# Two column blocks of an output projection by seven products of halves, with four sums of weights formed in DRAM during the recurrence before it

## The chip, the cores and the metric

The kernel runs on one core of one Trainium2 chip. The metric is device time in microseconds (us) of one execution; less is better. Before the change the median of three runs was 1098.96 us (1098.77 to 1100.81). Tile, line and engine names are those of the profile: PE is TensorE's matmuls, PEld its weight loads, DVE is VectorE, ACT is ScalarE, POOL is GpSimd, SP is the engine that only issues transfers. "L157" is line 157 of the kernel before.

## What is computed

One decoder layer on 512 tokens of 2048 channels. The stage that changes is the output projection with its residual; the rest is cut to a line each.

```python
h = rms_norm(x, norm_g)                      # 512 x 2048
z = h @ w_in                                 # 2048 x 6272: r, k, v, lora inputs, gates, pool input
y_rwkv = wkv7_scan(r, decay, k, v, kk, a)    # 16 heads of 64, a recurrence over the tokens
y_pool = pooled means of 2, 4, 8, 16 tokens @ w_pool
y_mix = concatenate([y_rwkv * silu(g), y_pool * scale * silu(g_pool)])   # 512 x 2048
x = x + y_mix @ w_out                        # the output projection, 2048 x 2048
x = x + sigmoid(x @ w_pg + b_pg) * (p @ w_ple)
out = rms_norm(x, final_g)
```

All is float32. The big products split each operand into a high part that TensorE multiplies exactly enough and the rest (`hi`, `lo`), and add three products: hi by hi, hi by lo, lo by hi. One "chunk" below is a 128 x 512 piece of a weight matrix, 256 KB.

## The kernel before

**Stages, in the order of time.** Norm and transposes of the input; the input projection, whose matmuls are kept in the order of the program and put between the steps of the recurrence, which goes over 8 pairs of heads with 8 "hops" each (one hop is one step of the state over 64 tokens; the state's scaled copy is `s0p`, L816, on POOL); the output projection `proj(w_out, ..., "o")`; the gate projection `proj(w_pg, ..., "g")`; the last norm.

**The weight chain.** `wsplit` (L129 to L133) loads a chunk into a tile `raw` by a transfer that SP issues, ACT copies it to `whi` (L132), and DVE subtracts for `wlo` (L133). The tiles `raw`, `whi` and `wlo` have 4 buffers each, so the load of a chunk can start when the subtraction of the chunk four places earlier has ended. SP's queue is issued in order: a load that waits for its buffer holds up all behind it.

**The output projection.** Four column blocks of 512 (`ec` 0 to 3). A block goes over the 16 chunks of the sum (`k`) in the list `order`; each chunk is used for 4 tiles of 128 tokens, three matmuls each, 12 matmuls in all of 512 columns (L157, `acc_o`). In block 0 the activations come on the way: `load_y` (L918, an ACT-issued transfer from the DRAM copy `yd`) fills one of six `yin` buffers, ACT makes `yhi` and DVE `ylo`, both whole tiles of 16 chunks. After a block, ACT-issued transfers bring the residual `x` (L994), DVE adds the four accumulators to it (L995), the sums go to DRAM (`x2d`, L996), and `turn` transposes the four tiles on PE (`px`, L1002, 16 transposes), splitting the result into `x2hi` and `x2lo`. Blocks 0, 1 and 2 are turned right behind their own matmuls, block 3 within the first gate block.

**What sets the order.** Each engine runs its own queue in order; a scheduler that records the program orders them by priorities from the program's text, with `tc.issue_after(...)` where an instruction must stand behind another and `tc.high_priority` where it may come early.

Of the kernel before, what the change touches and what calls it, by code (L numbers as in the profile page):

```python
# [9 lines left out]
F32 = mybir.dt.float32  # L10
# [5 lines left out]
P = 128  # L16
# [14 lines left out]
CK = 4  # L31


@with_exitstack
def trunk_kernel(ctx: ExitStack, tc: tile.TileContext, x, p, norm_g, w_in, mu, w0, w_up, a0, a_up,
# [87 lines left out]
    hhi = hp.tile([P, KT, T], F32R, name="hhi", tag="ahi")  # L123
    hlo = hp.tile([P, KT, T], F32R, name="hlo", tag="alo")


    def wsplit(src, kt, n, nm):
        raw = wp.tile([P, kt, n], F32, name=f"raw_{nm}", tag="raw")
        nc.sync.dma_start(out=raw, in_=src)  # L129
# [275 lines left out]
    def pool_unit(n):  # L405
# [32 lines left out]
        nc.scalar.dma_start(out=yd[NJ + m], in_=sgp)  # L438

# [316 lines left out]
    def recur(j, work, between):  # L756
# [17 lines left out]
        for ch in range(NCH):  # L774
# [25 lines left out]
            if ch < NCH - 1:  # L800
# [12 lines left out]
                if ch < NCH - 2:  # L813
                    for h in range(2):
                        hc = slice(64 * h, 64 * h + 64)
                        nc.gpsimd.tensor_scalar(s0p[hc, :], nxt[hc, hc], pcn[hc], None, ALU.mult)  # L816
# [56 lines left out]
    pending = []  # L873
    need("k", 0)
# [39 lines left out]
    AHEAD = 6  # L914

    def load_y(k):
        t_ = ymp.tile([P, T], F32, name=f"yin{k}", tag="yin", bufs=AHEAD)
        nc.scalar.dma_start(out=t_, in_=yd[k])  # L918
        split(yhi[:, k, :], ylo[:, k, :], t_)

# [6 lines left out]
    x2hi = hp.tile([P, KT, T], F32R, name="x2hi", tag="ahi")  # L927
    x2lo = hp.tile([P, KT, T], F32R, name="x2lo", tag="alo")
# [11 lines left out]
    def proj(w, hi_, lo_, ec, nm, ks=range(KT), tts=range(NT), keep=None, aside=None):  # L940
        acc = {tt: acc_tile(f"acc_{nm}{ec}_{tt}") for tt in tts}
        for i, k in enumerate(ks):
# [5 lines left out]
            elif nm == "o" and ec == 0 and i < 4:  # L948
                wh, wl = chunk(f"{nm}{ec}_{k}", 0)
            elif keep is None or LATE <= i < KT - KEEP:  # L950
                wh, wl = wsplit(src, 1, EC, f"{nm}{ec}_{k}")
            else:
# [12 lines left out]
                if i >= LATE:  # L965
                    continue
            for tt in tts if keep is None or i >= LATE else tts[:-1]:
# [3 lines left out]
            if aside is not None and i == 2:  # L971
                with tc.issue_after(e_.ins):
                    hi = aside()
                with tc.issue_after(hi.ins):
                    recall(0, lp)
# [11 lines left out]
    for ec in range(D // EC):  # L987
        es = slice(ec * EC, (ec + 1) * EC)
        acc = proj(w_out, yhi, ylo, ec, "o", order)
        x2 = []  # L990
        for tt in range(NT):
            rows = slice(tt * P, (tt + 1) * P)
            t_ = pp.tile([P, EC], F32, name=f"x2_{ec}_{tt}", tag=("u", "sw")[tt // 2])
            nc.scalar.dma_start(out=t_, in_=x[rows, es])  # L994
            nc.vector.tensor_tensor(t_, acc[tt], t_, ALU.add)  # L995
            nc.scalar.dma_start(out=x2d[rows, es], in_=t_)  # L996
            x2.append(t_)
        def turn(ec=ec, x2=x2):
            for i in range(EC // P):
                pt = psM.tile([P, T], F32, name=f"px2_{ec}_{i}", tag="m")  # L1000
                for tt in range(NT):
                    nc.tensor.transpose(pt[:, tt * P:(tt + 1) * P], x2[tt][:, i * P:(i + 1) * P], ident)  # L1002
# [178 lines left out]
```

## Time and profile before

| | |
|---|---|
| median of 3 runs | 1098.96 us |
| the profiled execution, by its own clock | 1097.72 us |
| its span in the profile | 1095.9 us |
| TensorE clock granted, mean | 0.998 |
| PE / DVE / ACT / POOL busy | 98% / 65% / 41% / 7% |
| output projection, four blocks | 728.97 to about 909 us of the span |

The span leaves out 1.8 us of the execution that lie around it. "Busy" of PE counts from the start of the first to the modelled end of the last of overlapping matmuls; a single matmul's duration is longer than the step from one to the next.

### The profile page before, as it was taken

The page shows a single profiled execution, that of the slowest core. Times are in us where ns is not written, and L with a number is a line of the kernel's source. Part 1 is how long each engine was busy: PE and PEld are TensorE (multiplying, and loading weights), DVE is VectorE, ACT ScalarE, POOL GpSimd, SP SyncE. Part 2 cuts the span into 40 slices and gives each one's busy share as a digit, 9 for nine tenths or more (in the row PEclk, how much of TensorE's full clock was granted, in tenths as well). Part 3 has the DMA queues.
Part 4 walks back from the last instruction along what each step waited for, and adds up shares of the span by engine and source line. Part 5 has one row for each costly group of instructions (what it writes and reads, how often), then busy time and mean ns, then how long its engine had stood idle before and what let it go on. Part 6 is the DMA issues. An engine that isn't in the chain of part 4 may idle for free.

```text
span 1095.9 us, 17196 instructions
## 1 busy us (share of the span) xinstructions
PE 1070.8 (98%) x6060; PEld 877.6 (80%) x6060; DVE 708.2 (65%) x1835; ACT 448.3 (41%) x917; POOL 76.9 (7%) x180
## 2 busy tenths in 40 slices
PE   5999999999999999999999999999999999999996
PEld 4888878887788888788878788888888888888885
DVE  6687867878688679678886956454433424445366
ACT  7633535345335335353343344543222222233337
POOL 2100110110110110100101101000000000000000
PEclk9999999999999999999999999999999999999999
DMA  7433433332423333333334242775534438455534
GB/s 233 116 96 97 111 92 84 96 100 73 120 82 105 104 92 89 96 82 93 91 94 119 79 138 93 232 233 169 172 124 136 167 99 244 137 189 137 181 106 154
DMA packets 178486, 138.56 MB, mean 126 GB/s; under 512 B 34678, under 2 KB 139743, under 8 KB 178399
## 3 DMA queue, kind: packets, MB, share of 16 engines
q1 hardware_dynamic: 157694, 103.89, 32.1%
q10 hardware_dynamic: 20704, 33.56, 9.8%
q8 instruction: 48, 0.79, 0.3%
q14 instruction: 40, 0.32, 0.1%
HBM read 118.02 MB, written 18.87 MB: 125 GB/s over the span
## 4 chain that ended last, share of the span: by engine, by line
PE 86%; DVE 5%; DMA 4%; ACT 3%; issue 1%; SPq 0%; ACTq 0%; DVEq 0%
PE acc_o L157 16%; PE zb L157 14%; PE acc_g L157 14%; PE zv L157 8%; PE zk L157 7%; PE zg L157 7%; PE zr L157 7%; PE py L157 2%; PE pple L157 2%; PE pm L157 1%; PE pu L157 1%; DMA n<-nd 1%; PE pp L157 1%; DMA raw_g<-in_w_pg_dram 1%; PE ps L157 1%
## 5 line engine op out<-in xcount | busy, mean ns | idle before, releaser
L133 DVE TENSOR_TENSOR wlo_g<-raw_g,whi_g 128x512 fp32r<-128x512 f32 x84 | 57.0, 685 | 79.6 <-ACT whi_g L132 76.5
L157 PE MATMUL zb<-hhi,whi_b 128*128 128x512 f32 x256 | 107.0, 418 | 0.0
L133 DVE TENSOR_TENSOR wlo_o<-raw_o,whi_o 128x512 fp32r<-128x512 f32 x64 | 43.9, 690 | 91.4 <-ACT whi_o L132 91.4
L157 PE MATMUL zb<-hhi,wlo_b 128*128 128x512 f32 x256 | 100.5, 393 | 0.0
L157 PE MATMUL acc_o<-whi_o,ylo 128*128 128x512 f32 x256 | 100.2, 391 | 0.0
L157 PE MATMUL acc_o<-whi_o,yhi 128*128 128x512 f32 x256 | 99.9, 390 | 0.0
L157 PE MATMUL zb<-hlo,whi_b 128*128 128x512 f32 x256 | 99.9, 390 | 0.0
L157 PE MATMUL acc_o<-wlo_o,yhi 128*128 128x512 f32 x256 | 99.8, 390 | 0.0
L132 ACT CAST whi_g<-raw_g 128x512 fp32r<-128x512 f32 x84 | 51.9, 620 | 102.7 <-PE acc_g L157 55.4
L157 PE MATMUL acc_g<-whi_g,x2hi 128*128 128x512 f32 x208 | 81.3, 391 | 0.0
L157 PE MATMUL acc_g<-wlo_g,x2hi 128*128 128x512 f32 x208 | 80.9, 389 | 0.0
L157 PE MATMUL acc_g<-whi_g,x2lo 128*128 128x512 f32 x208 | 80.7, 389 | 0.0
L132 ACT CAST whi_o<-raw_o 128x512 fp32r<-128x512 f32 x64 | 39.9, 623 | 97.0 <-PE acc_o L157 96.7
L816 POOL TENSOR_SCALAR s0p<-sbd,pw 64x64 f32<-64x64 f32 x96 | 56.6, 589 | 322.8 <-DVE sbd L809 255.0
L132 ACT CAST whi_b<-raw_b 128x512 fp32r<-128x512 f32 x64 | 39.7, 621 | 86.5 <-PE zv L157 35.4
L133 DVE TENSOR_TENSOR wlo_b<-raw_b,whi_b 128x512 fp32r<-128x512 f32 x64 | 43.8, 685 | 34.2 <-ACT whi_b L132 32.9
L157 PEld LDWEIGHTS zb<-hhi,wlo_b 128*128 128x128 f32 x256 | 48.0, 188 | 11.1
L661 DVE TENSOR_TENSOR xw<-xw,tm 128x60 f32<-128x60 f32 (+24 forms) x248 | 52.1, 210 | 6.8
L157 PEld LDWEIGHTS acc_o<-wlo_o,yhi 128*128 128x128 f32 x256 | 48.1, 188 | 10.3 <-DVE wlo_o L133 0.4
L157 PEld LDWEIGHTS acc_o<-whi_o,yhi 128*128 128x128 f32 x256 | 48.1, 188 | 9.7
L157 PEld LDWEIGHTS acc_o<-whi_o,ylo 128*128 128x128 f32 x256 | 48.1, 188 | 9.8
L157 PEld LDWEIGHTS zb<-hhi,whi_b 128*128 128x128 f32 x256 | 48.2, 188 | 8.5
(285 smaller groups left out, 2550.0 us busy)
## 6 DMA issues: line engine op xcount, KB each, us to landing
raw_b<-in_w_in_dram SPq DMA_DIRECT2D x64, 256.0 KB
raw_o<-in_w_out_dram SPq DMA_DIRECT2D x64, 256.0 KB
raw_g<-in_w_pg_dram SPq DMA_DIRECT2D x64, 256.0 KB
raw_k<-in_w_in_dram SPq DMA_DIRECT2D x32, 256.0 KB
raw_r<-in_w_in_dram SPq DMA_DIRECT2D x32, 256.0 KB
raw_v<-in_w_in_dram SPq DMA_DIRECT2D x32, 256.0 KB
raw_g<-in_w_in_dram SPq DMA_DIRECT2D x32, 256.0 KB
n<-nd SPq DMA_DIRECT2D x16, 256.0 KB
```

Source lines behind the costliest of these rows:

```text
L132: nc.scalar.copy(hi, raw)
L133: nc.vector.tensor_tensor(lo, raw, hi.bitcast(F32), ALU.subtract)
L157: i = nc.tensor.matmul(*a, **k)
L661: nc.vector.tensor_tensor(xw[:, 0:n_, s + 1:32], xw[:, 0:n_, s + 1:32], tm[:, 0:n_, 0:w_], ALU.add)
L816: nc.gpsimd.tensor_scalar(s0p[hc, :], nxt[hc, hc], pcn[hc], None, ALU.mult)
```

## The change

**1. Column blocks 1 and 2.** Write A for the activations and B for the weights of these two blocks. A is cut in two token halves (left, right 256) and two halves of the sum (even and odd chunks of a pair `q`); B in the same halves of the sum and in the two column blocks. Instead of eight products of halves, `seven(1, 2)` makes seven, in four phases of 128 x 512 chunks with six matmuls each:

| phase | products | weights |
|---|---|---|
| A | m3 = A11 (B12+B22), m4 = A22 (B21+B11) | sums 3 and 4, from DRAM |
| B | m1 = (A11-A22)(B11-B22), m5 = (A11-A12) B22 | plain chunks; for m1 DVE subtracts a second loaded tile `less` from `raw` before the split |
| C | m6 = (A21-A11)(B11+B12) onto m3, m7 = (A12-A22)(B21+B22) onto m4 | sums 6 and 7, from DRAM |
| D | m2 = (A22-A21) B11 | plain chunks |

Phases A, B and C use 16 chunks each, D uses 8. Then C12 = m3 - m5, C21 = m4 - m2, C11 = m1 + m5 + (m4 + m7), C22 = m1 + m2 + (m3 + m6), added by DVE with the residual between the phases. Residual loads and `x2d` stores of these two blocks go through POOL's queue.

**2. Sums of weights** (`sums_of`). 16 SP-issued copies of 512 KB from DRAM to DRAM, each followed three hops later by a POOL-issued transfer that adds another 512 KB in DRAM, one of each per hop that scales the state, in the second to the sixth pair of heads as the adding transfers stand.

**3. Differences of activations** (`sab_sums`). In block 0, for each pair of chunks, five DVE subtractions of 128 x 256 from the `yin` tiles, and splits by ACT and DVE into tiles `sh` and `sl`; the splits for m6, m7 and m2 are spread over later phases. To have room, `hhi`, `hlo`, `x2hi`, `x2lo` become four tiles each. The weights of block 0 from its fifth chunk on get a higher priority.

**4. Transposes.** Blocks 0, 1 and 2 are turned inside block 3 (after its chunks 0, 2 and 5); block 0's sums are read back from `x2d` for it. Block 3 is turned in the first gate block as before.

```diff
+    def sums_of(nm, w, c1, c2):
+        t_ = {m: dram.tile([KT // 2, P, EC], F32, name=f"sum_{nm}{m}", bufs=1) for m in (3, 4, 6, 7)}
...
+            for i in range(len(jobs_) + 3):
+                if i < len(jobs_):
+                    m, q, one, _ = jobs_[i]
+                    with tc.issue_after(behind[0].ins):
+                        nc.sync.dma_start(out=at(m, q), in_=pairs(w, *one, q))
+                if i >= 3:
+                    m, q, _, two = jobs_[i - 3]
+                    with tc.issue_after(behind[1].ins):
+                        nc.gpsimd.dma_start(out=at(m, q), in_=pairs(w, *two, q), accum_op=ALU.add)
...
-                        nc.gpsimd.tensor_scalar(s0p[hc, :], nxt[hc, hc], pcn[hc], None, ALU.mult)
+                        scaled_ = nc.gpsimd.tensor_scalar(s0p[hc, :], nxt[hc, hc], pcn[hc], None, ALU.mult)
+                    adds(loaded[0], scaled_)
...
+        two = pp.tile([P, 2, T // 2], F32, name=f"sr{q}", tag="sgp", bufs=1)
+        sraw[1, q], sraw[5, q] = two[:, 0, :], two[:, 1, :]
+        a11, a21, a12, a22 = a1[:, LH], a1[:, RH], a2[:, LH], a2[:, RH]
+        for m, p_, n_ in ((1, a11, a22), (5, a11, a12), (6, a21, a11), (7, a12, a22), (2, a22, a21)):
+            nc.vector.tensor_tensor(sraw[m, q], p_, n_, ALU.subtract)
+        sab_split(1, q)
+        sab_split(5, q)
...
+            raw = wp.tile([P, 1, EC], F32, name=f"raw_{nm}", tag="raw")
+            nc.sync.dma_start(out=raw, in_=src[0](q).unsqueeze(1))
...
+            tt_(raw, raw, less[-1][:, i % 2:i % 2 + 1, :], sub)
+            split(wh, wl, raw)
...
+        def run(parts, then=None):
+            for n_, q in enumerate(QO):
+                for src, ops, res, more in parts:
+                    wh, wl = weights(src, q)
+                    for a in range(2):
+                        xh, xl = ops(q, a)
+                        for i, (l_, r_) in enumerate(((xh, wh), (xh, wl), (xl, wh))):
+                            mm(res[a], l_, r_[:, 0, :], start=not more and n_ + i == 0,
+                               stop=n_ == KT // 2 - 1 and i == 2, skip_group_check=True)
...
-        acc = proj(w_out, yhi, ylo, ec, "o", order)
...
+    block_o(0, lambda tt: dict(pool=ymp, tag="cx", bufs=6))
+    x21, x22 = seven(1, 2)
+    x20 = recalled(0)
+    x23 = block_o(3, lambda tt: dict(pool=pp, tag=("u", "sw")[tt // 2]),
+                  {0: lambda: turn(0, x20), 2: lambda: turn(1, x21), 5: lambda: turn(2, x22)})
```

**How the order moves.** POOL, in the recurrence of the second pair of heads (`s0p` is the scaled state, `pw` the decay). Before:

```order
L660 COPY xw_2819<-i_116 128x256
L816 TENSOR_SCALAR s0p_0_2650<-sbd_567,pw_1440 64x64 x2
L816 TENSOR_SCALAR s0p_1_2805<-sbd_566,pw_1440 64x64 x2
L816 TENSOR_SCALAR s0p_2_2881<-sbd_567,pw_1440 64x64 x2
L816 TENSOR_SCALAR s0p_3_2954<-sbd_566,pw_1440 64x64 x2
```

Now:

```order
L719 COPY xw_2842<-i_116 128x256
L875 TENSOR_SCALAR s0p_0_2669<-sbd_573,pw_1450 64x64 x2
L875 TENSOR_SCALAR s0p_1_2826<-sbd_572,pw_1450 64x64 x2
L484 DMA sum_o_601<-in_w_out_dram 128x2x512
L875 TENSOR_SCALAR s0p_2_2904<-sbd_573,pw_1450 64x64 x2
```

The adding transfer stands between two hops' copies of the state, ahead of the next hop's `s0p`.

DVE, in the last third of block 0. Before (`wlo_o_7` is the weight chunk 7):

```order
L133 TENSOR_TENSOR wlo_o_4_8336<-raw_o_4_8333,whi_o_4_8335 128x512
L133 TENSOR_TENSOR wlo_o_5_8354<-raw_o_5_8351,whi_o_5_8353 128x512
L133 TENSOR_TENSOR wlo_o_6_8372<-raw_o_6_8369,whi_o_6_8371 128x512
L133 TENSOR_TENSOR wlo_o_7_8390<-raw_o_7_8387,whi_o_7_8389 128x512
L133 TENSOR_TENSOR wlo_o_14_8408<-raw_o_14_8405,whi_o_14_8407 128x512
L133 TENSOR_TENSOR wlo_o_15_8426<-raw_o_15_8423,whi_o_15_8425 128x512
```

Now (`sr`, `s6r`, `s7r`, `s2r` are differences of activations, `sl` their low parts):

```order
L150 TENSOR_TENSOR wlo_o_14_8532<-raw_o_14_8529,whi_o_14_8531 128x512
L155 TENSOR_TENSOR sl_8620<-s6r_8198,sh_8619 128x256
L155 TENSOR_TENSOR sl_8854<-s7r_8203,sh_8853 128x256
L155 TENSOR_TENSOR sl_8218<-sr_8415,sh_8217 128x256
L1006 TENSOR_TENSOR s6r_8198<-yin_8383 128x256
L1006 TENSOR_TENSOR sr_8461<-yin_8275,yin_8297 128x256 x2
L150 TENSOR_TENSOR wlo_o_15_8550<-raw_o_15_8547,whi_o_15_8549 128x512
L155 TENSOR_TENSOR ylo<-yin_8383,yhi 128x512
L155 TENSOR_TENSOR ylo<-yin_8405,yhi 128x512
```

The differences stand between the weights' subtractions, and the last two `ylo` come behind the block's last weight chunk.

DVE, between one product and the next. Before, from the block of columns 0 to that of columns 1 (`x_0_0` to `x_0_3` are the residual sums, `x2lo` the turn's low parts):

```order
L133 TENSOR_TENSOR wlo_o_9_8510<-raw_o_9_8507,whi_o_9_8509 128x512
L133 TENSOR_TENSOR wlo_o_10_8528<-raw_o_10_8525,whi_o_10_8527 128x512
L995 TENSOR_TENSOR x_0_0_8441<-acc_o_0_8133,x_0_0_8441 128x512
L995 TENSOR_TENSOR x_0_1_8445<-acc_o_1_8134,x_0_1_8445 128x512
L995 TENSOR_TENSOR x_0_2_8449<-acc_o_2_8135,x_0_2_8449 128x512
L995 TENSOR_TENSOR x_0_3_8453<-acc_o_3_8136,x_0_3_8453 128x512
L138 TENSOR_TENSOR x2lo<-px_0_0_8457,x2hi 128x512
L138 TENSOR_TENSOR x2lo<-px_0_1_8464,x2hi 128x512
L138 TENSOR_TENSOR x2lo<-px_0_2_8471,x2hi 128x512
L138 TENSOR_TENSOR x2lo<-px_0_3_8478,x2hi 128x512
L133 TENSOR_TENSOR wlo_o_11_8546<-raw_o_11_8543,whi_o_11_8545 128x512
```

Now, from phase B to phase C:

```order
L150 TENSOR_TENSOR wlo_f_9088<-raw_f_9085,whi_f_9087 128x512
L1190 TENSOR_TENSOR c_9055<-seven_8823,x_0_9056 128x512
L1191 TENSOR_TENSOR c_8805<-c_8805,seven_8823 128x512
L1196 TENSOR_TENSOR c_9055<-c_9055,c_9061 128x512
L1190 TENSOR_TENSOR c_9064<-seven_8824,x_1_9065 128x512
L1191 TENSOR_TENSOR c_8806<-c_8806,seven_8824 128x512
L1196 TENSOR_TENSOR c_9064<-c_9064,c_9070 128x512
L155 TENSOR_TENSOR sl_9098<-s2r_8200,sh_9097 128x256
L150 TENSOR_TENSOR wlo_f_9104<-raw_f_9101,whi_f_9103 128x512
```

`wlo_f_9088` is the second chunk of phase C and `wlo_f_9104` its third: six additions with the accumulators of phase B (`seven`) stand between them. A chunk lasts PE half as long here as before, six matmuls instead of 12.

192 lines of the change are left out of this document (167 added, 25 removed).

## The prediction

> **What bounds the kernel now.** I read the page's busy shares and its chain first, then the chain piece by piece over the output projection, then the groups of that stage and its waits, then transfers.
>
> ```profile
> PE 1070.8 (98%) x6060; PEld 877.6 (80%) x6060; DVE 708.2 (65%) x1835; ACT 448.3 (41%) x917; POOL 76.9 (7%) x180
> PE 86%; DVE 5%; DMA 4%; ACT 3%; issue 1%; SPq 0%; ACTq 0%; DVEq 0%
> 728.97 43.77 PE acc_o L157 x192
> 777.12 41.06 PE acc_o L157 x181
> L157 PE MATMUL acc_o<-whi_o,yhi 128*128 128x512 f32 x256 | 99.9, 390 | 0.0
> ACT whi_o L132 <- PE acc_o L157: 96.7, 47, 2.1
> ```
>
> PE is busy for nearly the whole span and the chain of what ended last is PE. In the output projection it is nothing else: the first block is one unbroken piece of 192 matmuls. What a matmul costs has to be read there: 43.77 / 192 = 0.228 us (the second piece gives 41.06 / 181 = 0.227). The group's 390 ns is the duration of one matmul while the next already runs, and 390 x 256 x 3 would be longer than the stage. The last line shows the room in the weight chain: 47 times the cast of a weight chunk waited, up to 2.1 us, for PE to free the `whi` buffer that it overwrites, so the weights were there before PE wanted them.
>
> **The gain.** Two plain blocks take 2 x 192 = 384 matmuls, the seven products 7 x 8 pairs x 6 = 336. The 64 transposes stay, elsewhere. 48 x 0.228 = 10.9 us less on PE, all of it on the path. With 390 ns it would have been 18.7, which the chain denies.
>
> **Weights twice as fast.** A chunk now feeds 6 matmuls, 6 x 0.228 = 1.37 us, where it fed 12 in 2.74. The four `raw` buffers make a cycle: load, cast, subtraction, load again. It must fit into four chunks, 4 x 1.37 = 5.47 us.
>
> ```profile
> L133 DVE TENSOR_TENSOR wlo_o<-raw_o,whi_o 128x512 fp32r<-128x512 f32 x64 | 43.9, 690 | 91.4 <-ACT whi_o L132 91.4
> L132 ACT CAST whi_o<-raw_o 128x512 fp32r<-128x512 f32 x64 | 39.9, 623 | 97.0 <-PE acc_o L157 96.7
> 1024.94 0.33 SPq L954 DMA_DIRECT2D raw_g<-in_w_pg_dram  x1
> 1028.97 0.62 ACT L137 CAST dhk<-raw_g 128x512 fp32r<-128x512 f32 x1 [2.05 <-DMA raw_g<-in_w_pg_dram]
> 1042.13 0.33 SPq L954 DMA_DIRECT2D raw_g<-in_w_pg_dram  x1
> 1045.51 0.62 ACT L137 CAST whik<-raw_g 128x512 fp32r<-128x512 f32 x1 [1.32 <-DMA raw_g<-in_w_pg_dram]
> 731.38 0.81 ACTq L918 DMA_DIRECT2D yin<-yd  x2
> 736.52 1.38 ACT L137 CAST yhi<-yin 128x512 fp32r<-128x512 f32 x2 [1.72 <-DMA yin<-yd]
> 737.34 0.81 ACTq L918 DMA_DIRECT2D yin<-yd  x2
> 740.05 1.31 ACT L137 CAST yhi<-yin 128x512 fp32r<-128x512 f32 x2 [1.24 <-DMA yin<-yd]
> 1028.00:1046.00 18.00, 17.89 (x79) 14.47 (x78) 8.88 (x14) 7.42 (x13) 0.00 (x0) 1.00 0.52 166
> 729.00:751.00 22.00, 22.00 (x97) 17.94 (x96) 13.91 (x22) 11.41 (x20) 0.00 (x0) 1.00 0.73 237
> 909.00:913.00 4.00, 4.00 (x20) 3.30 (x19) 1.39 (x3) 0.92 (x2) 0.00 (x0) 1.00 0.94 299
> 921.00:925.00 4.00, 4.00 (x19) 3.29 (x18) 1.38 (x3) 0.85 (x2) 0.00 (x0) 1.00 1.01 379
> ```
>
> No row gives the time of a weight load in the new stage, so it is bounded by loads of the same 256 KB that the next engine waited for: from issue to cast 4.03, 3.38, 5.14 and 2.71 us, mean 3.82. The load adds 0.62 for the cast and 0.69 for the subtraction: 5.13 us, within 5.47, but with only 0.34 to spare. In phase B the chunks of m1 have `raw - less` in front of the cast, another 0.69: 5.82, over by 0.35 for each of four rounds of four chunks, 1.4 us. Lateness does not average out, since a load late by more than the spare stops PE and an early one gives nothing back; for that I add 0.8. Bounds: at 2.71 nothing; at 5.14, 10 rounds (phases A, C, D, 40 chunks) x 0.98 and 4 rounds of B x 1.67 = 16.5. I take 2.2, by the mean of the rows.
>
> Is there bandwidth? Phase A moves 16 chunks (4.19 MB), the stores and residual loads between block 0 and the next (1.05 and 1.05) and two early `less` (0.5) in 16 x 1.37 = 21.9 us: 310 GB/s. Phase B, with 24 loads, 287. The window rows (last column GB/s, before it the transfer engines' share) show 237 with 0.73 busy while PE never stopped, and 299 to 379 at full share. So it fits, with little to spare. The Trainium skill ("DMA: Bandwidth & Descriptors", Anatomy of one DMA — SWDGE (gpsimd) path) fits a transfer as 2.0 us and its bytes over 436e3 per us. By that, as an estimate, 256 KB takes 2.6 us, below every row here, and the weight chain would cost nothing; the rows decide, since they were taken beside other transfers as these will be.
>
> **Block 0: DVE.** All `sab_sums`, and the splits for m1 and m5, fall here. From the first changed DVE row to the end of block 0's part there are 34 operations of 128x512 and 67 of 128x256.
>
> ```profile
> L133 DVE TENSOR_TENSOR wlo_wp<-raw_wp,whi_wp 128x256 fp32r<-128x256 f32 x8 | 3.3, 410 | 1.4 <-ACT whi_wp L132 1.4
> 771.32 2.48 DVE L995 TENSOR_TENSOR x<-acc_o,x 128x512 f32<-128x512 f32 x4
> 729.00:773.00 44.00, 44.00 (x196) 36.07 (x195) 21.12 (x33) 16.40 (x28) 0.00 (x0) 1.00 0.53 174
> ```
>
> At full durations 34 x 0.69 + 67 x 0.41 = 50.9 us, beside 43.8 of PE: 7.1 too many. But four operations in a row took 2.48, so one follows the next after (2.48 - 0.69) / 3 = 0.60; scaled alike the narrow ones follow after 0.36, and the sum is 44.5, 0.7 over. Part of the list runs before PE enters the block and part after it. The order puts `ylo` of the last two chunks behind the block's last weights, so a late DVE is felt at once. I take 1.5, nearer the second, between 0 and 7.1. ACT's casts (16.4 busy of 44) have room.
>
> **Starts of phases.** Only two chunks' `whi` and `wlo` lie ready, 2 x 1.37 = 2.74 us, while DVE empties accumulators. Into A: four sums stand ahead of the third chunk, but three end with earlier banks; from PE's end 0.60 + 0.60 + 0.69 = 1.9, covered. Into C: six additions, of which the last three wait for m5's second bank, the first three for the first, freed 3 x 0.228 = 0.68 earlier. 6 x 0.60 + 0.36 + 0.69 - 0.68 = 4.0 after PE's end, against 2.74: 1.2 us. Into D: six again, but only the last two wait for the last bank: covered, unless the residual is late. I take 2.0 for all, the rest for residuals that now come through POOL's queue; bounds 0.7 (C with 0.5 of cover more) and 3.6 (three starts at 1.2). Below nothing is excluded for all three terms so far: PE had no wait here that could go.
>
> **Recurrence.** 16 copies and 16 adding transfers.
>
> ```profile
> 290.00:440.00 150.00, 148.77 (x967) 121.00 (x966) 118.52 (x354) 63.53 (x140) 17.48 (x30) 1.00 0.34 95
> PE py L157 <- DVE sbd L809: 1.2, 2, 0.9
> 218.42 0.97 POOL L816 TENSOR_SCALAR s0p<-sbd,pw 64x64 f32<-64x64 f32 x2 [10.69 <-DVE sbd L809]
> 224.99 1.04 POOL L816 TENSOR_SCALAR s0p<-sbd,pw 64x64 f32<-64x64 f32 x2 [5.60 <-DVE sbd L809]
> 230.80 1.01 POOL L816 TENSOR_SCALAR s0p<-sbd,pw 64x64 f32<-64x64 f32 x2 [4.76 <-DVE sbd L809]
> 290.68 7.09 DMA n<-nd
> ```
>
> PE loses 1.2 us in 150; input-projection matmuls fill its waits. Transfer engines are a third busy. A copy of 512 KB at 340 GB/s (between the two full windows) holds a load behind it by 1.5 us, and there a chunk lasts 2.74 us, so the cycle has 4 x 2.74 - 5.13 = 5.8 to spare. POOL sits idle 4.76 to 10.69 us before each pair of `s0p`; an adding transfer whose issue takes less costs nothing, and no row shows that issue. What can be late is what is behind it on POOL, `s0p` and the copy into `xw`, whose chain has little slack at `n<-nd` (7.09 on the chain). I take 0.7; below, nothing or a gain of 0.3 (waits that fall differently), above 16 x 0.4 = 6.4 us if each costs what one row's wait does (half of 1.2 and less).
>
> **Nothing for** the moved turns (48 transposes inside block 3, beside matmuls that cover their splits: 4 x 0.60 in chunks of 2.74 us), the re-read of block 0's sums (early, POOL's queue free by then), and the four-part tiles.
>
> **Sum.** -10.9 + 2.2 + 1.5 + 2.0 + 0.7 = -4.5 us. The profiled execution, 1097.7 (span 1095.9 and 1.8 around it), becomes 1093.2; it lies 1.2 under the median of 1098.96, which becomes 1094.5. What can be told from no change here is about 0.2%, 2.2 us.
>
> **Rivals.**
> - *Weights late, slower.* At phases A to C the loads of a busy time become the rule. With a load of L the chain costs 10 (L - 4.16) + 4 (L - 3.47) us where both brackets are positive; with the other 4.2 us the gain is gone at L = 4.44, between the rows' 4.03 and 5.14. At 4.8 it is 11.7 + 4.2 - 10.9 = +5.0: 1104; at 5.14 +9.8: 1108.8. For it: demand of 290 to 310 GB/s, above the 237 of the window that had the 5.14. Against: PE was busy 4.00 of 4.00 us in the windows at 299 and at 379 GB/s.
> - *Everything fits.* Loads near 2.7 to 3.4 and a DVE at 0.60: only the starts at 0.7 and 0.3 of block 0 stay, -9.9: 1089.1. The fit of 2.6 us quoted from the skill would lead here. For it: 47 waits of the casts for PE. Against: those stand in blocks with half the pace.
> - *DVE bounds block 0.* At 7.1 instead of 1.5: +1.1 to 1100.1. For it: 50.9 us of work by durations; against: back-to-back rows at 0.60.
> - *The recurrence pays* for its 32 transfers, 6.4 instead of 0.7: 1100.2. The Trainium skill ("SBUF — State Buffer", SBUF: two separate sides) says that POOL cannot write the descriptors of its transfer while DVE holds the port they share, and DVE is 79% busy here. No run here has such a transfer. As a mechanism: POOL's queue held by more than 4.76 us sixteen times.
>
> **How the numbers follow.** Forecast 0.40 (1091 to 1098); weights late 0.25; everything fits 0.14; DVE 0.12; recurrence 0.09. Faster by over 0.2%: the forecast but 0.03, everything fits, 0.03 of the DVE and recurrence cases: 0.54. Slower: 0.22 of the weights and 0.07 of DVE and recurrence: 0.29. The rest 0.17. The range 1088.5 to 1105 leaves out about 0.04 below and 0.12 above, the loads over 4.8.
>
> **What would show it.** Step 1: 48 fewer `acc_o`-like matmuls, and phases A to D of 336 x 0.228 = 76.6 us plus stalls. Weight chain: in the waits, PE or its weight load waiting for `wlo_f` or `whi_f`, and ACT's cast of `raw_f` released by the transfer; right if most lie in phase B and sum to 2 to 3 us, wrong if A and C show them chunk after chunk. Block 0: longer than 43.8 by about 1.5, PE waiting for `ylo` near its end. Starts: a gap of 1 us at the third chunk of C. Recurrence: block 0 beginning within 1 us of 728.97. The prediction is wrong if loads take over 4.4 us on average, if DVE is still at block 0's work when A begins, or if block 0 begins some us late.

## The result and the profile after

| | before | after |
|---|---|---|
| median of 4 runs | 1098.87 us (1098.41 to 1100.81) | 1116.28 us (1109.06 to 1116.67) |
| ratio | | 1.014 [1.0097, 1.0182] |
| profiled execution, span | 1097.72, 1095.9 us | 1116.67, 1114.7 us |
| TensorE clock granted, mean | 0.998 | 0.993 |
| block 0 begins | 728.8 us | 740.6 us |
| block 0 | 43.8 us | 44.3 us |
| from its end to the gate projection | 136.3 us | 143.6 us |

The change makes the kernel slower by 1.4%, where -0.4% was forecast. Of the four runs after, one took 1109.06 us and the others 1116.23 to 1116.67; the profile is of the slowest. The page of the kernel after: the busy shares, and the engines on the chain.

```profile
PE 1070.0 (96%) x6012; PEld 871.5 (78%) x6012; DVE 761.9 (68%) x1959; ACT 477.3 (43%) x983; POOL 106.3 (10%) x216
PE 69%; DMA 12%; DVE 11%; ACT 4%; issue 2%; SPq 0%; ACTq 0%; DVEq 0%
```

The 48 matmuls are gone (6060 to 6012), yet PE is busy as long as before and its part of the chain fell from 86% to 69%: DMA and DVE now stand in the chain. They do so in two places, one ahead of the output projection and one in it.

**The recurrence, +11.8 us.** The chain of the second kernel enters block 0 through other work, so the first matmul on `acc_o` is compared: 740.6 against 728.8. The waits of POOL (200 to 700 us, the second row of that view) and of PE (60 to 735 us, the first row), and then POOL's rows in time order, with the copies that SP issues for them:

```profile
POOL sum_o L484 <- DMA sum_o<-in_w_out_dram: 111.6, 15, 17.1
PE py L174 <- DVE sbd L868: 10.4, 8, 3.5
```

```profile
219.83 0.97 POOL L875 TENSOR_SCALAR s0p<-sbd,pw 64x64 f32<-64x64 f32 x2 [10.68 <-DVE sbd L868]
229.86 1.40 POOL L484 DMA_DIRECT2D sum_o<-in_w_out_dram  x1 [9.06 <-DMA sum_o<-in_w_out_dram]
231.35 1.04 POOL L875 TENSOR_SCALAR s0p<-sbd,pw 64x64 f32<-64x64 f32 x2
233.22 1.06 POOL L875 TENSOR_SCALAR s0p<-sbd,pw 64x64 f32<-64x64 f32 x2 [0.84 <-DVE sbd L868]
```

```profile
220.01 0.64 SPq L480 DMA_DIRECT2D sum_o<-in_w_out_dram  x1
240.57 0.59 SPq L480 DMA_DIRECT2D sum_o<-in_w_out_dram  x1
```

The add is at the head of POOL's queue and waits 9.06 us there for the copy that SP issued at 220.01. The next `s0p` follows the add at once, with no idle time of its own: it was ready. Before, the same three pairs stood at 218.42, 224.99 and 230.80; now the middle one is at 231.35, 6.4 us later, where the first is 1.4 later. This happens 15 times, 111.6 us of POOL, and PE's wait for the state (`py`, 1.6 us before in the same window) becomes 10.4.

The three hops recorded between a copy and its add are not there in time. The first add (229.86) is issued before SP comes to its second copy (240.57): each add stands right behind its own copy, because all 16 copies stand in SP's queue right behind a load of weights that has to wait for its buffer. Two adds on POOL, and the copy on SP for the second:

```profile
257.19 1.20 POOL L484 DMA_DIRECT2D sum_o<-in_w_out_dram  x1 [0.50 <-DMA sum_o<-in_w_out_dram]
275.04 1.13 POOL L484 DMA_DIRECT2D sum_o<-in_w_out_dram  x1 [16.65 <-DMA sum_o<-in_w_out_dram]
270.09 0.59 SPq L480 DMA_DIRECT2D sum_o<-in_w_out_dram  x1
```

POOL is free for its next add at 258.39, SP issues the copy at 270.09, and the add is issued at 275.04. Of the 111.6 us, 37.1 lie before SP had issued the copy at all; from its issue a copy took 4.1 to 9.8 us to land.

**Phases A to D, +16.1 us.** From 784.9 to 877.7, where PE begins block 3, they take 92.7 us, where 336 x 0.228 = 76.6 was to be had. A takes 27.9 and B 27.3 instead of 21.9 each, C and D together 37.6 instead of 32.8. The matmul groups of PE in that stretch (the last columns are idle time just before them and who ended it), and pieces of the chain there:

```profile
L174 PE MATMUL seven<-wlo_f,sh 128*128 128x512 f32 x80 | 32.5, 407 | 5.8 <-DVE wlo_f L150 2.9 <-DVE wlo_f L155 2.7
L174 PE MATMUL seven<-whi_f,sh 128*128 128x512 f32 x80 | 31.5, 402 | 0.4 <-ACT whi_f L149 0.4
L174 PE MATMUL seven<-wlo_f,yhi 128*128 128x512 f32 x32 | 13.5, 421 | 1.6 <-DVE wlo_f L150 1.6
L174 PE MATMUL seven<-whi_f,yhi 128*128 128x512 f32 x32 | 13.1, 410 | 1.8 <-ACT whi_f L149 1.8
```

```profile
789.40 6.80 DMA raw_f<-sum_o
813.33 6.59 DMA raw_f<-in_w_out_dram
821.93 6.08 DMA raw_f<-in_w_out_dram
846.26 5.70 DMA raw_f<-sum_o
```

PE waits for the weights (`whi_f`, `wlo_f`) and behind these stand loads of 5.7 to 6.8 us (one more of 5.16 at 854.36); others on the same chain took 3.05 to 3.64. The long ones fall early in A and B and within C. Over all 56 weight loads of the phases, each taken from its issue to the last of its landing events, the mean is 4.12 us and the median 3.67, but eight in a row among A's, and six of seven in the middle of B's, took 4.2 to 6.8. What is there at the start of A: SP's, ACT's and POOL's issues, and then the windows of 4 us (the last three columns are TensorE's granted clock, the transfer engines' share, GB/s):

```profile
786.20 1.95 SPq L1135 DMA_DIRECT2D less<-in_w_out_dram  x2
789.40 8.59 SPq L146 DMA_DIRECT2D raw_f<-sum_o  x5
787.01 2.46 ACTq L1093 DMA_DIRECT2D x2d<-x  x4
793.36 1.62 POOL L1089 DMA_DIRECT2D x<-in_x_dram  x3 [15.03 <-DMA x2d<-x]
```

```profile
788.00:792.00 4.00, 2.60 (x11) 1.91 (x11) 3.47 (x7) 1.66 (x3) 0.00 (x0) 1.00 0.95 236
792.00:796.00 4.00, 3.13 (x14) 2.25 (x12) 0.13 (x1) 0.00 (x0) 1.62 (x3) 1.00 0.96 322
796.00:800.00 4.00, 2.81 (x8) 2.09 (x9) 2.01 (x3) 1.85 (x3) 0.54 (x1) 0.82 1.00 388
800.00:804.00 4.00, 4.00 (x15) 3.18 (x15) 2.12 (x4) 2.39 (x4) 0.00 (x0) 0.76 0.75 243
```

Two `less` loads, four stores, three residual loads and the weights share the transfer engines, at a share of 0.95 to 1.00 from 788 to 800. The clock falls to 0.82 and 0.76 right after PE's wait of 1.84 us at 796.97, a second cost of the same wait. PE's idle time in the four phases is 9.6 us (the shown groups'), the clock of 0.94 that the trace gives for A and for B costs some 3.0 (0.06 x 24.3 and 24.5 busy), and ten restarts at 0.50 us for a first matmul instead of 0.228 some 2.7; 0.8 stays unassigned.

Three of the ten stalls, 3.8 us, stand at the third chunk of a phase: 1.40 at 789.42 in A, 0.88 at 844.74 in C, 1.51 at 869.83 in D. There DVE comes late to a subtraction, as its rows at A and at D show:

```profile
785.95 0.42 DVE L155 TENSOR_TENSOR sl<-s7r,sh 128x256 fp32r<-128x256 f32 x1
786.29 2.48 DVE L1108 TENSOR_TENSOR x<-acc_o,x 128x512 f32<-128x512 f32 x4
788.68 0.68 DVE L150 TENSOR_TENSOR wlo_f<-raw_f,whi_f 128x512 fp32r<-128x512 f32 x1
868.49 0.68 DVE L1202 TENSOR_TENSOR c<-c,x 128x512 f32<-128x512 f32 x1
869.09 2.49 DVE L150 TENSOR_TENSOR wlo_f<-raw_f,whi_f 128x512 fp32r<-128x512 f32 x4
```

At A, DVE still splits differences made in block 0 until 786.3, begins the four additions that empty the accumulators only then, 1.2 us after the end of block 0's last matmul, and the third chunk comes behind them. At D six additions run from 865.49 on ahead of the third chunk.

**Block 3, +1.9 us.** With its 48 transposes it takes 50.8 us; one block and 48 transposes took 48.9 before (136.3 less two blocks of 43.7). PE waits 0.78 us at 880.19 for an accumulator that the additions behind D must empty first, and in kernels without that wait (in_order below) the block still takes 49.7.

Together 11.8 + 0.5 + 16.1 + 1.9 - 10.9 = 19.4, within 0.2 of the 19.6 us by which the gate projection begins later; behind it 0.8 came back.

### The profile page after: what moved, and what is told of

It reads as the page before. It is cut to its first block, busy times and chain, and to the rows that moved or that the text cites. A ratio compares the mean times of both kernels' runs of the same rounds, so it can differ in the third digit from the quotient of the medians.

```text
span 1114.7 us, 17497 instructions
## 1 busy us (share of the span) xinstructions
PE 1070.0 (96%) x6012; PEld 871.5 (78%) x6012; DVE 761.9 (68%) x1959; ACT 477.3 (43%) x983; POOL 106.3 (10%) x216
## 4 chain that ended last, share of the span: by engine, by line
PE 69%; DMA 12%; DVE 11%; ACT 4%; issue 2%; SPq 0%; ACTq 0%; DVEq 0%
PE acc_g L174 14%; PE zb L174 14%; PE zv L174 7%; PE zg L174 7%; PE zr L174 5%; PE zk L174 5%; PE acc_o L174 4%; DMA n<-nd 3%; DMA yin<-yd 3%; DMA raw_f<-in_w_out_dram 2%; PE py L174 2%; DMA raw_f<-sum_o 2%; PE pple L174 2%; PE pu L174 1%; PE seven L174 1%
## 5 line engine op out<-in xcount | busy, mean ns | idle before, releaser
L149 ACT CAST whi_b<-raw_b 128x512 fp32r<-128x512 f32 x64 | 39.7, 620 | 87.6 <-PE zv L174 32.8
L150 DVE TENSOR_TENSOR wlo_b<-raw_b,whi_b 128x512 fp32r<-128x512 f32 x64 | 43.8, 685 | 34.2 <-ACT whi_b L149 33.0
L716 DVE TENSOR_TENSOR tm<-xw,n 128x60 f32<-128x60 f32 (+10 forms) x240 | 50.6, 211 | 6.4
L174 PEld LDWEIGHTS zb<-hlo,whi_b 128*128 128x128 f32 x256 | 48.3, 189 | 7.9
L174 PE MATMUL zk<-hhi,whi_k 128*128 128x512 f32 x128 | 53.7, 419 | 0.0
L174 PE MATMUL zr<-hhi,whi_r 128*128 128x512 f32 x128 | 53.4, 418 | 0.0
L174 PE MATMUL zv<-hhi,whi_v 128*128 128x512 f32 x128 | 53.4, 417 | 0.0
L174 PE MATMUL zg<-hhi,whi_g 128*128 128x512 f32 x128 | 52.6, 411 | 0.0
L174 PE MATMUL acc_o<-whi_o,yhi 128*128 128x512 f32 x128 | 50.5, 395 | 0.8 <-DVE c L1208 0.8
L174 PE MATMUL zk<-hhi,wlo_k 128*128 128x512 f32 x128 | 50.9, 397 | 0.0
```

What stands on the lines that cost most here:

```text
L149: nc.scalar.copy(hi, raw)
L150: nc.vector.tensor_tensor(lo, raw, hi.bitcast(F32), ALU.subtract)
L174: i = nc.tensor.matmul(*a, **k)
L716: nc.vector.tensor_tensor(tm[:, 0:n_, 0:w_], xin[:, 0:n_, s:s + 1].to_broadcast([P, n_, w_]), nb[s // 16][:, s % 16:s % 16 + 1, s + 1:32]. ...
```

## The experiments

Theory: the recurrence pays because POOL stands in front of each add until its copy has landed, and the phases pay because loads come in bursts that four buffers, on half the time per chunk, cannot bridge. Rivals: the 32 transfers themselves slow the recurrence (by their issue or their bytes); the sums are slower to read from DRAM than weights; the order on DVE, not the loads, stops PE.

Each kernel is told by its edit against the kernel after, unless said otherwise. The columns "begins", "block 0" and "rest" are read from the profile: first matmul of block 0, its length, and the time from its end to the gate projection. The rest was 136.3 before; with 48 matmuls less it can be 125.4.

| kernel | median us (range, runs) | ratio to before | begins | block 0 | rest |
|---|---|---|---|---|---|
| later_adds | 1105.31 (1104.66 to 1105.72, 4) | 1.0061 [1.0045, 1.0078] | 731.7 | 44.1 | 141.3 |
| sums_only | 1105.78 (1102.53 to 1109.05, 4) | 1.0067 [1.0042, 1.0091] | 737.9 | 44.4 | 136.3 |
| plain_sums | 1105.21 (1104.66 to 1106.44, 4) | 1.0063 [1.0048, 1.0078] | 731.6 | 44.5 | 140.7 |
| raw8 | 1107.29 (1106.28 to 1109.03, 4) | 1.0082 [1.0067, 1.0097] | 737.0 | 48.3 | 135.9 |
| later_raw8 | 1104.33 (1103.62 to 1105.56, 4) | 1.0062 [1.0045, 1.0079] | 732.2 | 49.7 | 136.0 |
| later_order | 1099.74 (1096.49 to 1101.32, 10) | 1.0013 [1.0001, 1.0025] | 730.9 | 44.3 | 137.5 |
| later_raw8_order | 1101.05 (1099.30 to 1102.26, 7) | 1.0029 [1.0018, 1.0041] | 729.8 | 48.8 | 132.6 |
| quiet | 1097.45 (1094.80 to 1100.23, 10) | 0.9997 [0.9982, 1.0011] | 732.1 | 44.1 | 133.1 |
| in_order | 1098.34 (1096.15 to 1102.96, 12) | 1.0004 [0.9991, 1.0017] | 729.1 | 44.4 | 134.9 |
| in_order_spread | 1099.59 (1097.01 to 1105.57, 12) | 1.0018 [1.0003, 1.0034] | 731.1 | 45.0 | 134.8 |
| in_order_less_early | 1097.80 (1095.55 to 1100.19, 11) | 1.0002 [0.9991, 1.0014] | 731.7 | 45.2 | 132.8 |
| mended_no_less | 1096.29 (1094.80 to 1097.97, 10) | 0.9978 [0.9964, 0.9992] | 731.1 | 44.5 | 131.0 |
| mended_quiet | 1092.08 (1090.32 to 1095.04, 6) | 0.9940 [0.9918, 0.9962] | 730.6 | 44.4 | 127.1 |

The kernel before ran beside them with medians of 1098.66 us (the first four), 1098.23 (the next four), 1098.05 (in_order and in_order_spread), 1097.63 (in_order_less_early) and 1098.27 (the last two).

**later_adds: the add far behind its copy.** All transfers stay; each add is recorded 28 hops behind its copy instead of three.

```diff
-            for i in range(len(jobs_) + 3):
+            for i in range(len(jobs_) + 28):
-                if i >= 3:
-                    m, q, _, two = jobs_[i - 3]
+                if i >= 28:
+                    m, q, _, two = jobs_[i - 28]
```

> The changed kernel, with each adding transfer 28 hops behind its copy instead of 3, so that the copy has landed long before POOL comes to the add; nothing else. Theory P (POOL stands still in front of the add until its copy has landed, 4 to 9 us each time, and the state's scaled copy s0p behind it comes late): the recurrence loses nothing, the first block starts about 11 us earlier (near 729 to 731 us instead of 740.6), and the time falls from 1116.3 to about 1105. Rival T (the added bytes slow the loads and stores of the recurrence): the bytes are the same, so the time stays above 1113.

Block 0 begins at 731.7 instead of 740.6 and the median is 11.0 us lower; the rest is 2.3 shorter too, for which this edit gives no reason. The first rows of POOL's and of PE's waits in the same windows as above:

```profile
POOL s0p L875 <- DVE sbd L868: 208.7, 35, 12.0
PE py L174 <- DVE sbd L868: 4.6, 5, 1.8
```

No add waits for its copy any more, though 16 are still issued on POOL: the recurrence had paid for the wait, not for the transfer.

**sums_only: the kernel before, with the 32 transfers and no reader of their sums.**

```diff
+    osum, adds = sums_of("o", w_out, 1, 2)
...
+                    adds(loaded[0], scaled_)
```

> The kernel before, with the 16 copies and 16 adding transfers as in the changed kernel, whose result nothing reads. Theory P and rival T: slower than before by what the recurrence lost in the changed kernel, 11 to 12 us: about 1110.5. If the loss came from something else of the change (the quarter tiles, the priority of block 0's weights), about 1099.

POOL's second and PE's first row:

```profile
POOL sum_o L468 <- DMA sum_o<-in_w_out_dram: 115.0, 16, 16.9
PE py L159 <- DVE sbd L852: 8.6, 7, 3.1
```

The same wait appears in the old kernel, and block 0 begins 9.1 us later; the median rises by 7.1, less than the 11 to 12 that I had expected. So some 9 of the 11.8 belong to the adds. These sizes have a scatter: the kernel after, sums_only and raw8 (below) have the recurrence's queues in the same order on every engine and begin block 0 at 740.6, 737.9 and 737.0. No kernel here without that wait begins later than 732.2.

**plain_sums: no transfers at all.** Phases A and C read plain chunks of the weights, so the products m3, m4, m6 and m7 are others; PE's work is the same.

```diff
-    osum, adds = sums_of("o", w_out, 1, 2)
-            return lambda q: osum[m][q]
+            odd, c = {3: (0, c2), 4: (1, c1), 6: (0, c1), 7: (1, c1)}[m]
+            return lambda q: wrows(w_out, 2 * q + odd, c)
```

> The changed kernel without copies and adds: phases A and C read plain weight chunks in place of the sums (it leaves the four sums out, so that the products are others). The recurrence is that of before. Theory W (the weight chain: four raw buffers, and loads that take 5 to 7 us where stores, residuals and loads come together): the first block starts near 729, phases A to D still take about 95 us instead of 76.6, time about 1104.5. Rival S (chunks read back from the DRAM sums are slower to load than rows of the weights): phases A and C lose little, time below 1098.

Two things follow. Loads of the sums from DRAM are not slower than loads of weights (rest 140.7 against 141.3 in later_adds). And block 0 still begins 2.8 us late with no transfer added, so 2.8 of the 11.8 have another cause or are scatter (before_again, below).

**raw8: eight load buffers for the phases.** A `raw_f` is the load tile of a chunk in the phases. Every other one takes a buffer that is free at that time (of the tile `ple`); the adds stay as in the kernel after.

```diff
+            turns[0] += 1
+            if turns[0] % 2:
+                return lp.tile([P, 1, EC], F32, name=f"raw_{nm}", tag="ple", bufs=4)
+            return wp.tile([P, 1, EC], F32, name=f"raw_{nm}", tag="raw")
```

> The changed kernel with eight instead of four buffers for the raw chunks of the seven products (four of them borrowed from tiles that are first used in the gate projection). Theory W: loads are asked for up to eight chunks ahead, a load of 6.8 us no longer stops PE; phases A to D fall from 95 to about 80 to 84 us, the time to about 1102 to 1106. Rival B (the transfer engines cannot bring the bytes in time whatever the buffers): less than 4 us gained, time above 1112.

The rest falls from 143.6 to 135.9, and C and D have one stall of 0.41 us left; phases A to D take 86.2, more than the 80 to 84 expected. But block 0 now takes 48.3: with free buffers, SP issues loads for the phases ahead of block 0's own weights (SP's rows of raw8).

```profile
725.88 0.33 SPq L1135 DMA_DIRECT2D raw_f<-sum_o  x1
726.31 0.37 SPq L146 DMA_DIRECT2D raw_o<-in_w_out_dram  x1
726.73 1.00 SPq L1135 DMA_DIRECT2D raw_f<-sum_o  x2
728.36 0.33 SPq L146 DMA_DIRECT2D raw_o<-in_w_out_dram  x1
729.57 0.32 SPq L1135 DMA_DIRECT2D raw_f<-sum_o  x1
```

Block 0 then waits for `yhi` (0.39, 0.84 and 0.23 us at three places, where the kernel after waited for none) and, with the restarts, loses 4 us in all.

**later_raw8: both of these.**

> The later adds and the eight raw buffers together. Theory W (four raw buffers are too few for loads of 5 to 7 us): against later adds alone (1105.3) phases C and D lose nothing any more and A and B about half, 8 us in all: 1097. Rival B (the bytes cannot come faster, whatever the buffers): above 1102.

Missed by 7 us: the rest came as low as in raw8 (136.0) but block 0 took 49.7, by the same order on SP.

**later_order: later adds, and the phases' weights recorded with a priority.**

```diff
-                    wh, wl = weights(src, q)
+                    with tc.high_priority(offset=300):
+                        wh, wl = weights(src, q)
```

> The later adds, four raw buffers, and a higher priority for the weight chain of the seven products, so that on DVE the split of the third and later chunks stands ahead of or between the additions that empty the accumulators. Theory O (at the start of A, B and C the additions hold up the split and with it the next load): 1.4 to 2.7 us less at A, B and C each, 1100 to 1102. Theory W alone: the loads stay late with four buffers, 1104 to 1106.

Another 5 us or so against later_adds (3.8 of them in the rest): the casts and subtractions of weights now stand ahead of the additions that empty the accumulators and of the activations' splits. The stalls at the third chunk of C and of D are gone, and that of A is 0.79 us in place of 1.40.

**later_raw8_order: all three.**

> Later adds, eight raw buffers and the higher priority together. If W and O name the whole loss of the phases: they take about 78 to 80 us, the time is 1090 to 1093, below the kernel before. If something else bounds them (bytes, DVE's work in phase B): 1096 or more.

Missed by 8 or more. The rest is 132.6, so buffers (-5.3) and order (-3.8) add up, but block 0 again takes 48.8.

**quiet: later adds, four buffers, without two kinds of transfers.** Zeros stand for the second operand of m1, and `yhi` for the residual of the two blocks.

```diff
-                    nc.sync.dma_start(out=less[-1][:, g:g + 1, :], in_=src[1](QO[i + g]).unsqueeze(1))
+                nc.gpsimd.memset(less[-1], 0.0)
-            return residual(ec, tt, ymp, by=nc.gpsimd, tag="cx", bufs=6)
+            return yhi[:, ec, :].bitcast(F32)
```

> The later adds with four raw buffers, without the eight residual loads of the two blocks and without the loads of less (it leaves these out: other tiles stand in for the residual, and zeros that POOL writes for less), DVE's work as it was. Theory C (loads are long because the residual loads, less and the stores come at the same time): loads of the weights take 3 to 4 us at A's and B's starts, 6 to 9 us gained, 1096 to 1099. Theory W without C (the load alone is too long for four buffers): above 1102.

7 to 8 us less than later_adds (8.2 in the rest), with the order and the buffers as they were, and the mean clock is 0.998 again. The 56 weight loads took 3.45 us on average against 3.99 in later_adds, and four in a row of A's that took 6.0 to 6.3 there took 3.6 to 3.7. So the long loads of the phases are made long by the transfers beside them: 2.1 MB of `less` and 2.1 MB of residuals.

**in_order: all three mends, and every load of the phases chained behind block 0's last.**

```diff
+        def load(out, in_):
+            with tc.issue_after(last[0].ins):
+                last[0] = nc.sync.dma_start(out=out, in_=in_)
```

> Later adds, eight raw buffers, higher priority, and the loads of the seven products kept in the order of the program behind block 0's last weight load, so that none of them runs ahead of block 0. Theory E (the extra buffers cost 5 us in block 0, since loads for the seven products went out before block 0's own and its activations came late): block 0 takes 44 us instead of 48.8, the time falls from 1101 to 1095 to 1097. If the stalls in block 0 have another cause: 1100 to 1102.

Block 0 is at 44.4, so raw8's loss there was the order of SP's queue; the rest is 2.3 us longer than in later_raw8_order, so half of what block 0 gets back is lost behind it. The median is some 1.3 us above what I expected. Now `less` comes late (DVE's row):

```profile
790.61 0.69 DVE L1152 TENSOR_TENSOR raw_f<-raw_f,less 128x512 f32<-128x512 f32 x1 [4.75 <-DMA less<-in_w_out_dram]
791.22 1.29 DVE L155 TENSOR_TENSOR wlo_f<-raw_f,whi_f 128x512 fp32r<-128x512 f32 x2
```

With a priority, phase B's first subtraction stands in DVE's queue ahead of splits for phase A, and both wait for its `less`; PE stops 1.82 us at 791.96 for the `wlo_f` of A.

**in_order_spread: the residual loads on SP, behind a load in the middle of the phase.**

```diff
-            return residual(ec, tt, ymp, by=nc.gpsimd, tag="cx", bufs=6)
+            with tc.issue_after(mid[0].ins):
+                return residual(ec, tt, ymp, by=nc.sync, tag="cx", bufs=6)
```

> As the one before, and the residual loads of the seven products go through SP's queue behind the ninth chunk of the phase, not through POOL's as soon as their tile is free. Theory C (weight loads are long because stores, less and residual loads come in the same few us at the starts of A and B): 1.5 to 4 us less than the kernel with the loads in order alone, 1091 to 1095, below the kernel before. If the total of bytes counts and not their moment: no change.

Missed: no gain, and the wait for `less` grew, with a stall of 2.84 us at 795.56 in place of 1.82.

**in_order_less_early: in_order, with the `less` loads outside the chain.**

> As the kernel with the loads in order, but the loads of less are free to go early again. In that kernel DVE stood 4.75 us in front of the first raw - less, waiting for less, with the splits of phase A behind it. Theory D (that wait, and nothing of the weights themselves, is A's second stall of 1.8 us and starts B late): 2 to 4 us less than 1098.3, 1094 to 1096, below the kernel before. If the transfers are what is short, whatever their order: within 1.5 us of 1098.3.

Missed: 0.5 us less than in_order, where 2 to 4 were expected. It has the lowest median of the versions that compute everything, and is no different from before: 1.0002 [0.9991, 1.0014]. What is left sums up: 2.9 us at the begin, 1.4 in block 0 and 7.4 in the rest, against the 10.9.

**before_again: the kernel before once more, profiled.**

> The kernel before, profiled once more, on another occasion. The first block's start was 728.8 in its first profile and 731.6 in the changed kernel without any sums. If it lies between 729 and 732 here too, those 2.8 us are the spread of the kernel before and not a cost of the change; if it is 728.8 within 0.3 us, the change costs them in some other way than by the sums.

1096.55 us, block 0 at 728.8 as in the first profile. The 2.8 us of plain_sums are thus no scatter of these two profiles of the kernel before. In plain_sums PE waits for `sbd` at the places where before hardly does (1.55 us at 452.36), though the instructions of the recurrence stand in the same order on every engine; and in_order began at 729.1. The ten kernels from later_adds on that share the later adds have the same order in every queue of the recurrence and begin between 729.1 and 732.2, 3.1 us apart. So the 2.8 can be scatter of the changed kernels, or a cost of about 2 us on average; the profiles here do not tell.

**mended_no_less: in_order_less_early with zeros for `less`; mended_quiet: also `yhi` for the residual.** The edits are those of quiet, first one, then both.

> The best mended kernel (later adds, eight raw buffers, priority, loads in order, less early; 1097.8), without the eight pairs of loads of less (it leaves them out: POOL writes zeros instead, and DVE's subtraction stays). If the 2.1 MB of less are what still crowds phase B and the end of A: 2 to 4 us less, 1094 to 1096. If it is DVE's extra subtraction, or the residuals: within 1 us of 1097.8.

> The same without less and without the eight residual loads of the two blocks as well (left out: another tile stands in). If bytes that come at the wrong time are the rest of the loss, phases A to D come within 2 us of 76.6 and the time is 1089 to 1092, and the full 10.9 us are then shown to be there. If DVE's longer chain in phase B and the starts of the phases bound it: 1094 or more.

Without `less` the rest is 131.0, and the median lies 1.5 us lower, between the two forecasts. Without both it is 127.1, and that kernel is 0.6% faster than before, which still loads its residuals. All waits of PE from 735 to 905 us in mended_quiet, and its stretches (block 0, A, then B to the gate projection):

```profile
PE seven L174 <- DVE wlo_f L155: 0.8, 1, 0.8
PE acc_o L174 <- DVE ylo L155: 0.6, 1, 0.6
```

```profile
730.60:774.90 44.30, 43.73 (x193) 35.92 (x192) 39.01 (x91) 24.99 (x57) 1.12 (x2) 1.00 0.62 205
775.00:797.90 22.90, 22.09 (x97) 17.89 (x96) 17.51 (x31) 11.16 (x19) 2.61 (x3) 1.00 0.71 229
797.90:902.00 104.10, 104.01 (x481) 85.70 (x480) 63.07 (x104) 44.40 (x78) 6.62 (x12) 1.00 0.56 175
```

PE is busy 104.01 of 104.10 us from phase B on. The seven products do give most of what the count of matmuls says (9.2 of 10.9 us in the rest), once POOL's queue, the order on SP and DVE, the buffers and 4.2 MB of transfers are out of the way. A kernel that computes the reference needs what these 4.2 MB bring. Bringing the residuals at another time was tried once (in_order_spread), without a gain; forming `less` in DRAM like the four sums was not tried.

## Why the prediction was wrong

**The gain: right.** 48 matmuls less, at 0.228 each: the kernel after shows 26.56 us for 117 matmuls of block 3 in its chain (0.227), and mended_quiet comes to 127.1 in the rest, where 136.3 - 10.9 = 125.4 was the least. What went wrong is the price of four other steps.

**Recurrence: the step that failed worst, 0.7 for 11.8.** The step said "an adding transfer whose issue takes less costs nothing, and no row shows that issue", and priced the issue. The issue measured 1.13 to 1.40 us, below the 4.76 it was held against, and later_adds shows that it costs next to nothing. What was left out is that the add waits for its copy to land, and that a wait is paid in the queue where it stands. That wait is 8.9 of the 11.8 (later_adds, one profile of each); the other 2.9 are open. The order quoted ahead of the prediction showed it: `sum_o` between two pairs of `s0p`. That a copy would go out three hops ahead of its add was taken from the program's text; SP's queue, which issued it right ahead of the add, had no term. The step did name what stands behind the add (`s0p`, the copy into `xw`), but charged it with the issue only. The rival's mechanism, "POOL's queue held by more than 4.76 us sixteen times", is what happened in part (111.6 / 15 = 7.4 us on average), at a price above its 6.4; the cause named beside it was another. By the Trainium skill ("SBUF — State Buffer", SBUF: two separate sides) DVE and POOL can lock each other out at a shared port. The trace bears out no such cost here: with DVE busy for 310 of the 400 us from 180 on, the 16 issues lie within 0.27 us of each other.

**Weights: 2.2 for about 11.** Seven of the ten stalls do not stand at a third chunk: 5.8 us, 1.9 with them for restarts, and the 3.0 of the clock. The mechanism was named, and so was the point, L = 4.44, at which the gain is gone. The mean itself was little off: the loads took 4.12 us on average against the 3.82 assumed, under 4.44, and with 4.12 the step's own formula gives 4 x (4.12 - 3.47) + 0.8 = 3.4. The step that failed is that one mean stands for every load, with 0.8 for the scatter. Of the 56 loads, 21 took more than 4.16 us, up to 6.80, and they came in runs, so that four buffers in turn were late. Taking each load's own excess over 4.16 (3.47 for m1's chunks) and a quarter of it, for four buffers, gives 7.8 us, an estimate from the trace.

The four rows had been taken where the transfer engines were between 52% and 73% busy; from 788 to 800 they ran at 95% to 100%. The demand was worked out, 310 GB/s over phase A, but as a mean over 22 us; stores, `less` and residuals came inside 12 us, and the windows that "fit" at 299 and 379 GB/s had a chunk per 2.74 us to feed, not per 1.37. Phase B was to bear the most; A lost as much, 6.0 against 5.4. The fit of 2.6 us in the Trainium skill ("DMA: Bandwidth & Descriptors", Anatomy of one DMA — SWDGE (gpsimd) path) is one for transfers that POOL issues; these loads are SP's, and the trace does not agree with it as their price: 2.54 us at the least, 4.12 on average.

**Starts: 2.0 for about 4.6.** The three stalls at a third chunk are 3.8 us, and 0.8 for their restarts. C's 1.2 was right (0.88). A and D were called covered and were not, 1.40 and 1.51: at A none of the four additions began before block 0's last matmul had ended, since DVE was still at block 0's work until 786.3, and at D the six stood ahead of the third chunk. The order of DVE is worth 3.8 in the rest (later_order).

**Moved turns: nothing for 1.9.** Block 3 with its 48 transposes takes 50.8 us for 48.9: a wait of 0.78 us for the accumulators with its restart, and some 0.8 that stay in every changed kernel.

**Block 0, DVE: 1.5 for 0.5.** The packed rate of 0.60 us for an operation was the right end; the 7.1 was not, though DVE carried 1.2 us of this work into phase A. PE's one wait for `ylo` (0.47 us at 779.80) stood where it was said to.

**What no step had:** the clock. The two longest waits of the phases, 1.84 and 2.74 us, were each followed by 3.4 us of slower matmuls, some 3 us in all.

**The range** ended at 1105, so that two rivals could not be true together. Weights (+5 to +9.8) and recurrence (+6.4) hang on nothing in common and both came: 1108.8 + 5.7 = 1114.5 with the terms as priced. That this lies near the measured 1116.28 is in part luck: the loads were not 5.14 us on average, and the recurrence cost more than 6.4.

## What to carry to other kernels

A transfer that must wait for another transfer is a wait of the engine that issues it: put it where the engine has nothing else in its queue for as long as the first may take to be issued and to land, and read both queues, not the distance in the program (later_adds: 8.9 us of the recurrence for one number). When a change doubles the rate at which weights are used, the peak of all transfers in one round of the buffers decides, not the mean over the stage, and load times must be taken from windows with the transfer engines as full as they will be. Fewer products can mean more bytes: here the phases load 56 chunks and 8 of `less` where two plain blocks loaded 32, 8.4 MB more, and after every other mend 4.2 MB of loads in these phases (`less`, and residuals that the kernel before loads too) still cost 5.7 us.

## What the runs showed of the hardware

**The clock after short gaps.** Windows of 4 us that hold or follow a stall of PE, of the kernel in_order (1.82 us at 791.96 and 2.08 at 809.58) and of raw8 (1.75 us at 804.30):

```profile
792.00:796.00 4.00, 4.00 (x11) 3.14 (x12) 2.40 (x4) 0.62 (x1) 0.00 (x0) 0.58 0.64 203
809.00:813.00 4.00, 3.42 (x8) 2.72 (x9) 3.73 (x7) 0.62 (x1) 0.54 (x1) 0.59 0.86 283
```

```profile
803.00:807.00 4.00, 2.70 (x12) 2.25 (x13) 3.65 (x6) 0.62 (x1) 0.00 (x0) 1.00 0.39 129
```

PE is busy 4.00 of 4.00 us at 792 and gets 11 matmuls done instead of some 18. In the output projection, stalls of 1.82, 1.84, 2.04, 2.08, 2.74 and 2.84 us were followed by a lower clock, 0.50 for 3.4 us where the window is laid on it, and those of 1.40 and 1.75 were not. The length of the stall alone does not decide it: in the recurrence stalls of 1.84 (at 386.0) and 1.88 us (461.0) of the kernel after, and one of 2.29 us in sums_only, were followed by a full clock. The windows after the last and after the stall at 796.97:

```profile
458.70:462.70 4.00, 4.00 (x20) 3.30 (x21) 3.69 (x15) 1.07 (x4) 0.47 (x2) 1.00 0.77 237
798.50:801.90 3.40, 3.40 (x10) 2.66 (x9) 1.52 (x3) 1.24 (x2) 0.00 (x0) 0.50 0.94 332
```

The Trainium skill ("TensorE: Matmul & The Clock Gate", What's actually happening) puts the fall behind an idle window of about 3.4 us; here single gaps of little more than half of that sufficed in some places and not in others.

**An adding transfer in DRAM.** 512 KB took 1.13 to 1.40 us of POOL to issue and 6.3 to 8.0 us to land (the page's row of the kernel after):

```profile
sum_o<-in_w_out_dram POOLq DMA_DIRECT2D x16, 512.0 KB, 6.8
```

By itself it did not disturb the recurrence measurably, as later_adds shows: block 0 began at 731.7, and at 731.6 in plain_sums without any sums, with a scatter of some 3 us between profiles.
